# Row sums of a 64 MB tensor: which rows of DRAM the first and the last loads read

## The chip, the cores and the metric

The kernel runs on one core of a Trainium2 chip. The metric is the device time of one execution in microseconds (us), as the median of several runs; lower is better. "The profile" is a record of one execution by the hardware profiler. Engines are named as it names them: DVE is VectorE, ACT is ScalarE, POOL is GpSimd, SP is SyncE, which here only issues transfers (SPq is its queue, ACTq that of ScalarE).

## The reference

```
x: (32, 512, 1024) float32
return np.sum(x, axis=-1).astype(np.float32)      # (32, 512)
```

There are 32 x 512 = 16,384 rows of 1,024 numbers (4 KB each), and each is summed. 64 MB are read, 64 KB are written.

## The kernel before

The rows are spread over the 128 partitions of the on-chip memory, J = 128 rows to each. Two regions of DRAM are laid out differently. `x_a` is the first 2,048 rows: partition p has 16 neighbouring rows, so that partitions are 64 KB apart. `x_b` is the rest: partition p has LONG = 112 neighbouring rows, so that partitions are 448 KB apart. The outputs `out_a` and `out_b` follow the same split. `rows_from(j, n)` gives n rows of every partition from column j on: columns 0 to 111 are `x_b`, 112 to 127 are `x_a`. The tile `sums` (128 x 128) holds the sum of column j in its column j.

Loads come in this order, all of them issued by SP through `rows` (L191):

- first a short load of FIRST = 7 rows per partition, columns 96 to 102 of `x_b`. It is moved to the entry of the program by `issue_first_load_at_entry`.
- then seven loads of 16 rows, 8 MB each (`wholes`): the whole of `x_a`, then columns 0 to 95 of `x_b`. The buffer pool `in` has three buffers. The second load of all is held until ScalarE has done a first tiny activation (`ready`), the third until VectorE has summed the first seven rows (`first`).
- then the last nine rows, columns 103 to 111 of `x_b`: one load of 6 rows, one of 2, and the last row in two halves of 512 numbers (L236, L237).

VectorE sums the short load and the first six of the large ones with one `tensor_reduce` each (L152). The last large load and the nine last rows are summed row by row, by VectorE with an add of a row's two halves that accumulates (`halves`, L166) and by ScalarE with an accumulating copy (`act`, L179). The very last row is summed in two steps, as its halves arrive.

There are three stores (L202). Two are issued by ScalarE once VectorE is done with the load of two rows: `out_b` columns 0 to 95 (384 bytes per partition) and all of `out_a` (64 bytes per partition). The third is issued by SP at the very end: `out_b` columns 96 to 111 (64 bytes per partition, 448 bytes apart). `wait_for_the_store_at_the_clear` lets the closing round of the engines go ahead and has only GpSimd's clearing of the semaphores wait for this third store.

Of the kernel before, what the change touches and what calls it, by code (L numbers as in the profile page):

```python
# [100 lines left out]
@with_exitstack  # L101
def kernel(
    ctx: ExitStack,
    tc: tile.TileContext,
    x: bass.AP,
    out: bass.AP,
):
    nc = tc.nc
    nc.at_finalize(issue_first_load_at_entry)
    nc.at_finalize(order_waits)  # L110
    nc.at_finalize(wait_for_the_store_at_the_clear)
    fp32 = mybir.dt.float32
    P = 128
    batch, seq, dim = x.shape
    rows = batch * seq
    J = rows // P
    BIG = 16

    LONG = J - BIG
    rows_in = x.flatten_outer_dims()
    rows_out = out.rearrange("b s -> (b s)")
    x_a = rows_in[: P * BIG].rearrange("(p j) d -> p j d", p=P)
    x_b = rows_in[P * BIG :].rearrange("(p j) d -> p j d", p=P)
    out_a = rows_out[: P * BIG].rearrange("(p j) -> p j", p=P)
    out_b = rows_out[P * BIG :].rearrange("(p j) -> p j", p=P)


    def rows_from(j, n):
        return x_b[:, j : j + n, :] if j < LONG else x_a[:, j - LONG : j - LONG + n, :]

    last = LONG - BIG
    FIRST = 7
    pieces = (512, 512)
    LINE = 64

    with (
        tc.tile_pool(name="small", bufs=1) as smallpool,  # L140
        tc.tile_pool(name="in", bufs=3) as inpool,
        tc.tile_pool(name="unread", bufs=4, space=bass.MemoryType.PSUM) as upool,
        tc.tile_pool(name="stage", bufs=1) as stpool,
        tc.manual_schedule(),
    ):


        seed = smallpool.tile([P, LINE // 2], fp32)
        sums = stpool.tile([P, J], fp32)

        def vec(dst, src):
            return nc.vector.tensor_reduce(  # L152
                out=dst, in_=src, axis=mybir.AxisListType.X, op=mybir.AluOpType.add
            )

        def hold(inst, until, reason):
            tc.add_manual_dep(
                inst.ins,
                until.ins.name,
                mybir.DependencyInfo(mybir.DependencyClass.Sync, mybir.DependencyReason.DATA),  # L160
                reason=reason,
            )

        def halves(dst, src):
            n = src.shape[-1] // 2
            return nc.vector.tensor_tensor_reduce(  # L166
                out=src[:, :n],
                in0=src[:, :n],
                in1=src[:, n:],
                scale=1.0,  # L170
                scalar=0.0,
                op0=mybir.AluOpType.add,
                op1=mybir.AluOpType.add,
                accum_out=dst,
            )

        def act(dst, src, n):
            unread = upool.tile([P, dim], fp32)
            nc.scalar.activation(  # L179
                out=unread[:, :n],  # L180
                in_=src,
                func=mybir.ActivationFunctionType.Copy,
                accum_out=dst,
            )

        sums_of = []

        def rows(t, a, n, j, n_act, pairs=False):
            nv = n - n_act
            block = t[:, a * dim : (a + n) * dim].rearrange("p (n d) -> p n d", d=dim)  # L190
            load = nc.sync.dma_start(out=block, in_=rows_from(j, n))  # L191
            if pairs:
                for q in range(nv):
                    sums_of.append(halves(sums[:, j + q : j + q + 1], block[:, q, :]))
            else:
                sums_of.append(vec(sums[:, j : j + nv], block[:, :nv, :]))
            for q in range(nv, n):
                act(sums[:, j + q : j + q + 1], block[:, q, :], dim)
            return load

        def store(eng, dst, j0, j1):
            return eng.dma_start(out=dst, in_=sums[:, j0:j1])  # L202

        nc.vector.memset(seed[:, :1], 0.0)  # L204
        unread = upool.tile([P, dim], fp32)
        ready = nc.scalar.activation(  # L206
            out=unread[:, :1], in_=seed[:, :1], func=mybir.ActivationFunctionType.Copy
        )

        j = last  # L210
        t = inpool.tile([P, BIG * dim + LINE], fp32)
        rows(t, 0, FIRST, j, 0)
        first = sums_of[-1]
        wholes = [LONG, *range(0, last, BIG)]
        for k, at in enumerate(wholes):
            t = inpool.tile([P, BIG * dim + LINE], fp32)
            if k < len(wholes) - 1:
                load = rows(t, 0, BIG, at, 0)
            else:
                rows(t, 0, BIG, at, 7, pairs=True)  # L220
            if k == 0:
                hold(load, ready, "no second load while the first one's descriptors are made")
            if k == 1:
                hold(load, first, "no descriptors of later loads while the first ones start")

        t = inpool.tile([P, BIG * dim + LINE], fp32)
        rows(t, FIRST, 6, j + FIRST, 2, pairs=True)
        two = rows(t, FIRST + 6, 2, j + FIRST + 6, 1, pairs=True)
        a = BIG - 1

        j += a
        c, width = pieces
        whole = t[:, a * dim + c : BIG * dim + 2]
        nc.vector.memset(whole[:, width + 1 :], 0.0)  # L234
        part = t[:, a * dim : a * dim + c]
        nc.sync.dma_start(out=part, in_=rows_from(j, 1)[:, 0, :c])  # L236
        nc.sync.dma_start(out=whole[:, :width], in_=rows_from(j, 1)[:, 0, c:])  # L237
        late = "its packets come behind those of the loads"
        hold(store(nc.scalar, out_b[:, :last], 0, last), two, late)
        hold(store(nc.scalar, out_a, LONG, J), two, late)  # L240
        halves(whole[:, width : width + 1], part)
        halves(sums[:, j : j + 1], whole)
        store(nc.sync, out_b[:, last:], last, LONG)


# [28 lines left out]
```

## Time and profile before

| what | value |
|---|---|
| median of 3 runs | 161.25 us (161.15 to 161.28) |
| the profiled execution | 161.23 us |
| its span, first to last instruction | 159.4 us |
| DVE busy | 120.6 us, 76% of the span |
| ACT busy | 12.1 us, 8% |
| transfers | 2160 packets, 67.18 MB, mean 421 GB/s over the span |

The span is what the profile sees of the execution; the difference to the execution's own time, 1.8 us, lies outside it. Busy shares are over the whole span. A transfer is split over 16 DMA engines; a packet here is what one partition gets of one transfer. A line such as `t<-in_x_dram SPq DMA_DIRECT2D x1, 3584.0 KB, 10.8` is a transfer from DRAM into a tile, issued once by SP, with its size and the microseconds from its issue to its landing.

### The profile page before, as it was taken

The page shows a single profiled execution, that of the slowest core. Times are in us where ns is not written, and L with a number is a line of the kernel's source. Part 1 is how long each engine was busy: PE and PEld are TensorE (multiplying, and loading weights), DVE is VectorE, ACT ScalarE, POOL GpSimd, SP SyncE. Part 2 cuts the span into 40 slices and gives each one's busy share as a digit, 9 for nine tenths or more (in the row PEclk, how much of TensorE's full clock was granted, in tenths as well). Part 3 has the DMA queues.
Part 4 walks back from the last instruction along what each step waited for, and adds up shares of the span by engine and source line. Part 5 has one row for each costly group of instructions (what it writes and reads, how often), then busy time and mean ns, then how long its engine had stood idle before and what let it go on. Part 6 is the DMA issues. An engine that isn't in the chain of part 4 may idle for free.

```text
span 159.4 us, 135 instructions
## 1 busy us (share of the span) xinstructions
DVE 120.6 (76%) x41; ACT 12.1 (8%) x22; POOL 0.2 (0%) x4
## 2 busy tenths in 40 slices
DVE  0029600499985999779995899949999499994955
ACT  3000000000000000000000000000000000003993
POOL 0000000000000000000000000000000000000000
DMA  8999989699699699699699797996996996996983
GB/s 302 396 486 526 411 378 526 280 510 526 263 526 526 263 526 526 263 526 493 296 526 444 345 526 345 444 526 280 510 526 263 526 526 263 526 526 265 425 376 134
DMA packets 2160, 67.18 MB, mean 421 GB/s; under 512 B 624, under 2 KB 624, under 8 KB 880
## 3 DMA queue, kind: packets, MB, share of 16 engines
q1 hardware_dynamic: 1872, 67.12, 97.8%
q10 hardware_dynamic: 288, 0.06, 0.2%
HBM read 67.11 MB, written 0.07 MB: 421 GB/s over the span
## 4 chain that ended last, share of the span: by engine, by line
DMA 71%; DVE 27%; SPq 1%; issue 0%; DVEq 0%
DMA t<-in_x_dram 71%; DVE sums L152 26%; SPq L191 0%; SPq L236 0%; DVE t L166 0%; DVEq L269 0%
## 5 line engine op out<-in xcount | busy, mean ns | idle before, releaser
L152 DVE TENSOR_REDUCE sums<-t 128x16 f32<-128x16384 f32 (+1 forms) x7 | 110.9, 15848 | 32.3 <-DMA t<-in_x_dram 32.3
L179 ACT ACTIVATE unread<-t 128x1024 f32<-128x1024 f32 x10 | 10.1, 1010 | 144.2 <-DMA t<-in_x_dram 144.2
L166 DVE CUSTOM_DVE_ANT_0 t<-t 128x512 f32<-128x512 f32 (+2 forms) x16 | 9.6, 656 | 4.0 <-DMA t<-in_x_dram 4.0
L179 ACT ACTIVATION_READ_ACCUMULATOR unread<-t 128x1 f32 x10 | 1.9, 186 | 0.0
L206 ACT ACT_TABLE_LOAD x1 | 1.3, 1283 | 0.8 <-PEq L258 0.8
L166 DVE DVE_READ_ACCUMULATOR2_ANT sums<- 128x1 f32 x15 | 1.3, 84 | 0.0
L204 DVE MEMSET seed<- 128x1 f32 x1 | 0.1, 59 | 0.8 <-PEq L258 0.8
L206 ACT ACTIVATE unread<-seed 128x1 f32<-128x1 f32 x1 | 0.2, 174 | 0.0
L258 POOL MEMSET const-bfloat16-1.0<- 128x1 bf16 x1 | 0.1, 101 | 0.0
L258 POOL MEMSET const-uint8-127<- 128x1 uint8 x1 | 0.1, 101 | 0.0
L258 POOL MEMSET const-float32-0.0<- 128x1 f32 x1 | 0.1, 98 | 0.2 <-issue 0.2
L258 POOL MEMSET const-float32-1.0<- 128x1 f32 x1 | 0.1, 98 | 0.0
L166 DVE DVE_READ_ACCUMULATOR2_ANT t<- 128x1 f32 x1 | 0.1, 81 | 0.0
L234 DVE MEMSET t<- 128x1 f32 x1 | 0.1, 59 | 0.0
## 6 DMA issues: line engine op xcount, KB each, us to landing
t<-in_x_dram SPq DMA_DIRECT2D x1, 3584.0 KB, 10.8
t<-in_x_dram SPq DMA_DIRECT2D x1, 3072.0 KB, 28.7
t<-in_x_dram SPq DMA_DIRECT2D x1, 1024.0 KB, 30.8
t<-in_x_dram SPq DMA_DIRECT2D x2, 256.0 KB, 31.0
t<-in_x_dram SPq DMA_DIRECT2D x7, 40.7
out_dram<-sums ACTq DMA_DIRECT2D x1, 48.0 KB, 1.6
out_dram<-sums ACTq DMA_DIRECT2D x1, 8.0 KB, 1.7
out_dram<-sums SPq DMA_DIRECT2D x1, 8.0 KB, 1.4
```

What stands on the lines that cost most here:

```text
L152: return nc.vector.tensor_reduce(out=dst, in_=src, axis=mybir.AxisListType.X, op=mybir.AluOpType.add)
L166: return nc.vector.tensor_tensor_reduce(out=src[:, :n], in0=src[:, :n], in1=src[:, n:], scale=1.0, scalar=0.0, op0=mybir.AluOpType.add, op ...
L179: nc.scalar.activation(out=unread[:, :n], in_=src, func=mybir.ActivationFunctionType.Copy, accum_out=dst,)
L204: nc.vector.memset(seed[:, :1], 0.0)
L206: ready = nc.scalar.activation(out=unread[:, :1], in_=seed[:, :1], func=mybir.ActivationFunctionType.Copy)
L234: nc.vector.memset(whole[:, width + 1 :], 0.0)
L258: nc = _bacc.Bacc("TRN2", target_bir_lowering=False, num_devices=1)
```

## The change

The rows of a partition are cut into three regions of DRAM instead of two. The first seven columns are `x_f`, the first 896 rows of the tensor: partition p has 7 neighbouring rows, and partitions are 28 KB apart. The last nine columns are `x_l`, the last 1,152 rows: partition p has 9 neighbouring rows, and partitions are 36 KB apart. Between them lies `x_b`, as before with 112 rows a partition, 448 KB apart, and all seven large loads read it. The columns of `sums` are now in the order of the loads. The sizes and the order of the loads, the engines that sum the rows and the holds stay as they are.

There is again one store for each region: from ScalarE `out_b` (448 bytes per partition) and `out_f` (28 bytes per partition, end to end), and at the end from SP `out_l` (36 bytes per partition, end to end in one piece of 4,608 bytes).

```diff
-    LONG = J - BIG
+    FIRST, LATE = 7, 9
+    LONG = J - FIRST - LATE
     rows_in = x.flatten_outer_dims()
     rows_out = out.rearrange("b s -> (b s)")
-    x_a = rows_in[: P * BIG].rearrange("(p j) d -> p j d", p=P)
-    x_b = rows_in[P * BIG :].rearrange("(p j) d -> p j d", p=P)
-    out_a = rows_out[: P * BIG].rearrange("(p j) -> p j", p=P)
-    out_b = rows_out[P * BIG :].rearrange("(p j) -> p j", p=P)
-
+    x_f, x_b, x_l = (
+        rows_in[P * at : P * (at + n)].rearrange("(p j) d -> p j d", p=P)
+        for at, n in ((0, FIRST), (FIRST, LONG), (FIRST + LONG, LATE))
+    )
+    out_f, out_b, out_l = (
+        rows_out[P * at : P * (at + n)].rearrange("(p j) -> p j", p=P)
+        for at, n in ((0, FIRST), (FIRST, LONG), (FIRST + LONG, LATE))
+    )
+
+
+    late_at = FIRST + LONG
 
     def rows_from(j, n):
-        return x_b[:, j : j + n, :] if j < LONG else x_a[:, j - LONG : j - LONG + n, :]
-
-    last = LONG - BIG
-    FIRST = 7
+        if j < FIRST:
+            return x_f[:, j : j + n, :]
+        if j < late_at:
+            return x_b[:, j - FIRST : j - FIRST + n, :]
+        return x_l[:, j - late_at : j - late_at + n, :]
+
...
-        j = last
         t = inpool.tile([P, BIG * dim + LINE], fp32)
-        rows(t, 0, FIRST, j, 0)
+        rows(t, 0, FIRST, 0, 0)
         first = sums_of[-1]
-        wholes = [LONG, *range(0, last, BIG)]
+        wholes = range(FIRST, late_at, BIG)
...
-        rows(t, FIRST, 6, j + FIRST, 2, pairs=True)
-        two = rows(t, FIRST + 6, 2, j + FIRST + 6, 1, pairs=True)
+        a = BIG - LATE
+        rows(t, a, 6, late_at, 2, pairs=True)
+        two = rows(t, a + 6, 2, late_at + 6, 1, pairs=True)
         a = BIG - 1
 
-        j += a
+        j = J - 1
...
-        hold(store(nc.scalar, out_b[:, :last], 0, last), two, late)
-        hold(store(nc.scalar, out_a, LONG, J), two, late)
+        hold(store(nc.scalar, out_b, FIRST, late_at), two, late)
+        hold(store(nc.scalar, out_f, 0, FIRST), two, late)
         halves(whole[:, width : width + 1], part)
         halves(sums[:, j : j + 1], whole)
-        store(nc.sync, out_b[:, last:], last, LONG)
+        store(nc.sync, out_l, late_at, J)
```

## The prediction

> **What bounds the kernel now.** I read the page first, then a table of windows cut at the landings of the loads, then the transfers in a window at either end. Everything here is one profiled execution of 159.4 us span.
>
> The page, in parts 1, 3, 4 and 6 (engines: busy us, share, count; queues: packets, MB, share of 16 engines; the chain that ended last; transfers: size, us from issue to landing):
>
> ```profile
> DVE 120.6 (76%) x41; ACT 12.1 (8%) x22; POOL 0.2 (0%) x4
> ...
> q1 hardware_dynamic: 1872, 67.12, 97.8%
> ...
> DMA 71%; DVE 27%; SPq 1%; issue 0%; DVEq 0%
> ...
> t<-in_x_dram SPq DMA_DIRECT2D x1, 3584.0 KB, 10.8
> ...
> out_dram<-sums ACTq DMA_DIRECT2D x1, 48.0 KB, 1.6
> out_dram<-sums ACTq DMA_DIRECT2D x1, 8.0 KB, 1.7
> out_dram<-sums SPq DMA_DIRECT2D x1, 8.0 KB, 1.4
> ```
>
> The queue of the loads fills 97.8% of 16 DMA engines' span. VectorE's 27% of the chain is only the chain walking back through a buffer's release; the transfers run on under it, as the windows show (columns: window, length, busy DVE, ACT, POOL with counts, clock, DMA share, GB/s):
>
> ```profile
> 10.77:30.11 19.34, 7.62 (x1) 0.00 (x0) 0.00 (x0) 1.00 1.00 434
> 30.11:49.50 19.39, 17.22 (x1) 0.00 (x0) 0.00 (x0) 1.00 1.00 433
> 49.50:68.85 19.35, 17.22 (x1) 0.00 (x0) 0.00 (x0) 1.00 1.00 434
> 68.85:88.16 19.31, 17.22 (x1) 0.00 (x0) 0.00 (x0) 1.00 1.00 434
> ```
>
> Each window runs from one landing of a 16-row load to the next. The DMA share is 1.00 in all four and a reduction takes 17.22 us of 19.3: the DMA engines never pause, VectorE has about 2 us to spare per tile. So the time is (first packet) + (bytes at 434 GB/s) + (what the first and last packets lose) + (the work after the last landing). Only those ends can move the result, unless an address pattern changes the 434.
>
> The first end, the transfers from 0 to 3 us (40 slices of 0.075 us):
>
> ```profile
> DMA  0000000000000999900090000980000000809989
> ...
> DMA packets 30, 0.86 MB, mean 287 GB/s; under 512 B 0, under 2 KB 0, under 8 KB 0
> ```
>
> The first packet starts in slice 13, at 0.98 us. The first load's 3584 KB are 3.67 MB, which at 434 GB/s take 8.46 us. It lands at 10.77. After its last packet a transfer still takes 0.37 us to land (found below). So 10.77 - 0.98 - 8.46 - 0.37 = 0.96 us go missing when the stream starts. The trace's records of single packets say where: the first packet of each of the 16 engines takes 1.06 to 1.96 us, every later packet of the same 28,672 bytes 1.06 to 1.07. The engines that start early are the slow ones, and all 16 finish their first packet between 2.6 and 3.04 us.
>
> The other end, the last instructions in order of time (start, us):
>
> ```profile
> 157.25 0.43 DVE L166 CUSTOM_DVE_ANT_0 t<-t 128x257 f32<-128x257 f32 x1 [0.21 <-DMA t<-in_x_dram]
> 157.60 0.08 DVE L166 DVE_READ_ACCUMULATOR2_ANT sums<- 128x1 f32 x1
> 157.71 0.35 SPq L202 DMA_DIRECT2D out_dram<-sums  x1
> ```
>
> The last piece lands at 157.22, VectorE needs 0.45 us, the store is issued at 157.71. By the packet records its packets run from 158.55 to 158.76 and it lands at 159.13, 0.37 us after the last packet. Semaphore clearing ends the span at 159.44.
>
> **The change part by part.** Instruction for instruction nothing is added or removed: 12 loads of 128 descriptors with the same sizes in the same order (7, seven times 16, 6, 2 and two half rows), the same reductions, the same three stores on the same queues with the same holds. What moves is where in DRAM they read and write.
>
> *The seven 16-row loads.* Before, the first of them read `x_a`, where partitions are 64 KB apart; the other six read `x_b`, 448 KB apart. After, all seven are 448 KB apart. The table above has both: 19.34 us for the neighbouring region, 19.31 to 19.39 for the strided ones. Cost: 0.
>
> *The last nine rows.* Partitions go from 448 KB apart to 36 KB apart. Packet records: 24,576 bytes take 912 ns, 8,192 take 309, 2,048 take 84, with no spread at all within a load; these are the DMA engine's own times. The nearest rows again say that distance changes nothing in a running stream. Cost: 0.
>
> *The first seven rows.* Partitions go from 448 KB to 28 KB apart, in the one place where the stream is not yet steady. No row shows a cold start from neighbouring rows. From below: if the whole excess came from 16 engines asking for far-apart addresses at once, it goes: -0.96 us. From above: if neighbouring rows collide more than distant ones, I bound it by the excess once more, +0.96. The nearest rows are the 64 KB and 448 KB windows, which agree within 0.1 us, and they say 0; but they are warm. Also, the two engines that start last (at 1.90 and 1.97) have nearly undisturbed first packets, 1.14 and 1.06 us, and one of them is the last engine to finish the loads, at 156.88; the earliest finishes at 156.51. So healing the slow first packets of the early engines alone brings nothing; the late starts must move too. I take -0.1. Whatever is gained here arrives at the end one for one, since the engines run back to back.
>
> The Trainium skill, "DMA: Bandwidth & Descriptors", section "Latency and other measured facts", reports that rows a large power of two apart in HBM lower the rate: 207 GB/s per direction at 512 KiB against 214 with padding. 448 KB is no such power, and this trace shows 433 to 434 GB/s on either layout. If the page's 3% did apply to the first load, an estimate from it would be 0.03 x 8.46 = 0.25 us gained.
>
> *The stores on ScalarE's queue.* 384 bytes per partition become 448, and 64 become 28. Packet records: 22 ns for 384 bytes, 10.5 for 64, eight packets per engine, so well under 0.1 us either way. They are covered: SP looks at their semaphores from 158.11 on, and the round of all engines that follows is over at 158.80, while the clear waits until 159.13 for the last store. The second store lands at 158.07 and is looked at at 158.24, so its landing may slip by 0.17 + 0.33 = 0.5 us before it costs anything. Cost: 0; without the cover, its slip.
>
> *The last store.* This one has no cover: the clear waits for it. [...] The packets cannot cost more than now (84 ns per engine). [...] The second store has neighbouring 64-byte pieces and lands 0.37 us after its last packet, like the strided one, so neighbourhood alone is free. Upper bound: the 0.37 us doubled, +0.37. Lower bound: 9 columns instead of 16 save nothing that I can find beyond 0.05, half the packet time. I take +0.05.
>
> *Sum.* 159.44 - 0.1 + 0.05 = 159.4 us of span. The profiled execution took 161.23, 1.79 outside the span, and the median of the three runs is 161.25. 159.39 + 1.79 = 161.18, and with the 0.02 to the median 161.2. A measurement of this kernel can tell about 0.2%, 0.32 us, from no change, so this counts as no change.
>
> **The rivals.**
>
> *The start heals (faster).* The first packets slow each other because of their addresses. For it: the 16 first packets are slow together and recover together at 3.0 us, which looks like a shared resource rather than a fixed latency, since late starters take 1.06. Against it: two engines start 0.9 us late, and addresses in a steady stream make no difference. Half of the excess gives 161.25 - 0.48 = 160.75; all of it 160.3. The point from which it decides: all 16 engines must finish their first packet by about 2.7.
>
> [...] The Trainium skill, same page, section "Specifications", says that a transfer under 512 B is done by read-modify-write; all three stores are below that before and after, so by that rule alone nothing changes.
>
> *The start gets worse (slower).* 16 engines in one region of 3.5 MB collide where they were spread over 56 MB. Up to the excess again: half of it 161.7, all of it 162.2. Against it: `x_a`, 8 MB in one piece, runs at 434 GB/s.
>
> *The change does not do what it says.* Not plausible here: the diff changes plain address arithmetic, and the descriptors (128 pieces per transfer) have the same form as those of `x_a` and `out_a` now.
>
> **How the numbers follow.** No measurable change 0.42: the nearest rows all say zero. The healed start 0.33: it is the only large unexplained loss in the kernel, and the change touches it. The store's price over 0.32 us 0.15, the worse start 0.10, together 0.25. The likeliest case gives 161.2, with its own range of 160.95 to 161.55. The wide range takes in half of the healed start and more (160.5) and the doubled landing with some of a worse start (161.8); what lies beyond, a start healed by more than three quarters or worsened by more than half, is about 0.15 to 0.2.
>
> **What would show it.** The windows between landings of 16-row loads should stay at 19.3 us and 434 GB/s; if one moves, my claim on distance falls. The first load's landing, 10.77 now, is the test of the start: 10.7 as I have it, 10.3 or less for the faster rival, 11.2 or more for the worse start. [...] From the last load's landing to the store's issue 0.49 us should stay. If the span moves with all of these unchanged, the prediction was wrong in a way that I did not think of.

## The result and the profile after

The changed kernel takes 161.55 us (median of 20 runs, 161.32 to 161.76) against 161.19 us (20 runs, 161.10 to 161.42): a ratio of 1.002, 95% interval 1.0014 to 1.0026. It is slower by 0.36 us, small but clear of the noise. The forecast was no measurable change, at 161.2.

The profiled execution took 161.50 us with a span of 159.7. First the page's lines on transfers (size, us from issue to landing):

```profile
t<-in_x_dram SPq DMA_DIRECT2D x1, 3584.0 KB, 11.3
...
out_dram<-sums ACTq DMA_DIRECT2D x1, 56.0 KB, 1.6
out_dram<-sums ACTq DMA_DIRECT2D x1, 3.5 KB, 1.5
out_dram<-sums SPq DMA_DIRECT2D x1, 4.5 KB, 1.4
```

The first load lands at 11.3 instead of 10.8; the stores take what they took. The stream between the landings of large loads (window, length, busy engines, clock, DMA share, GB/s):

```profile
11.29:30.58 19.29, 7.62 (x1) 0.00 (x0) 0.00 (x0) 1.00 1.00 435
30.58:49.90 19.32, 17.22 (x1) 0.00 (x0) 0.00 (x0) 1.00 1.00 434
49.90:69.26 19.36, 17.22 (x1) 0.00 (x0) 0.00 (x0) 1.00 1.00 433
```

It is the same stream, between 0.07 us faster and 0.01 slower per load than the windows before, which took 19.31 to 19.39. The transfers of the first 3 us (40 slices of 0.075 us):

```profile
DMA  0000000000000999900000090000000000089899
...
DMA packets 27, 0.77 MB, mean 258 GB/s; under 512 B 0, under 2 KB 0, under 8 KB 0
```

27 packets have begun instead of 30. The trace's records of single packets show three engines that lag: their first packets take 2.30 to 2.42 us, where before the slowest took 1.96. All 16 engines were through their first packet at 3.04 before; now the last is at 3.54. And the end:

```profile
157.51 0.43 DVE L175 CUSTOM_DVE_ANT_0 t<-t 128x257 f32<-128x257 f32 x1 [0.19 <-DMA t<-in_x_dram]
157.87 0.08 DVE L175 DVE_READ_ACCUMULATOR2_ANT sums<- 128x1 f32 x1
157.98 0.35 SPq L211 DMA_DIRECT2D out_dram<-sums  x1
```

The first landing is 0.52 us late. The last piece is 0.27 us late (157.49 against 157.22), so about half of the delay is made up on the way. The trace also records when each of the 16 shares of a load lands. Three shares are late at the first load (11.07, 11.18 and 11.29 us, the thirteenth at 10.78; before, all four came within 0.02), and three are still late at the last piece (157.31, 157.41 and 157.49, the thirteenth at 157.16). From the last landing on, everything costs what it did (0.49 us to the store's issue, 1.42 to its landing, as before), and the span is 0.27 us longer.

### The profile page after: what moved, and what is told of

It reads as the page before. It is cut to its first block, busy times and chain, and to the rows that moved or that the text cites. A ratio compares the mean times of both kernels' runs of the same rounds, so it can differ in the third digit from the quotient of the medians.

```text
span 159.7 us, 135 instructions
## 1 busy us (share of the span) xinstructions
DVE 120.5 (75%) x41; ACT 12.1 (8%) x22; POOL 0.2 (0%) x4
## 4 chain that ended last, share of the span: by engine, by line
DMA 71%; DVE 27%; SPq 1%; issue 0%; DVEq 0%
DMA t<-in_x_dram 71%; DVE sums L161 26%; SPq L200 0%; SPq L245 0%; DVE t L175 0%; DVEq L278 0%
## 5 line engine op out<-in xcount | busy, mean ns | idle before, releaser
L188 ACT ACTIVATE unread<-t 128x1024 f32<-128x1024 f32 x10 | 10.1, 1011 | 144.5 <-DMA t<-in_x_dram 144.5
## 6 DMA issues: line engine op xcount, KB each, us to landing
t<-in_x_dram SPq DMA_DIRECT2D x1, 3584.0 KB, 11.3
```

The lines of the kernel that those rows point to most:

```text
L188: nc.scalar.activation(out=unread[:, :n], in_=src, func=mybir.ActivationFunctionType.Copy, accum_out=dst,)
```

## The experiments

**Which part costs.** The layout was made a list of regions in DRAM order, each with the columns it holds; loads, holds and the columns of the three stores stay as in the changed kernel.

```diff
-    x_f, x_b, x_l = (...)          # and out_f, out_b, out_l
+    for cols in REGIONS:
+        n = sum(hi - lo for lo, hi in cols)
+        src = rows_in[P * at : P * (at + n)].rearrange("(p j) d -> p j d", p=P)
+        dst = rows_out[P * at : P * (at + n)].rearrange("(p j) -> p j", p=P)
...
# changed kernel:     [[(0, 7)], [(7, 119)], [(119, 128)]]
# e1_first_only:      [[(0, 7)], [(7, 119), (119, 128)]]
# e2_last_only:       [[(0, 7), (7, 119)], [(119, 128)]]
# e3_one_region_16:   [[(0, 7), (119, 128)], [(7, 119)]]
# e4_first_elsewhere: [[(7, 119)], [(0, 7)], [(119, 128)]]
```

> Only the first seven columns are a region of neighbouring rows (28 KB apart); the other 121 columns are one region, 484 KB apart, the last nine included. Theory 'spacing' (the first load starts worse because its partitions lie close together): first load lands at about 11.3 us as in the changed kernel, time 161.5 us. Theory 'the end' (the nine neighbouring rows or the small stores cost it): first load still about 11.3 or not, but time 161.2 us.

Measured: 161.55 us (ratio to before 1.0020, interval 1.0011 to 1.0029), first load 11.19 in the profiled execution, as in all that follows. The changed kernel's whole loss is there with the first region alone.

> Only the last nine columns are a region of their own (36 KB apart, stored as 36 bytes end to end); the first seven are with the 112 others, 476 KB apart. Theory 'spacing': first load lands at about 10.8 us, time 161.2 us. Theory 'the end': time 161.5 us.

Measured: 161.31 us (1.0004, 0.9995 to 1.0013), first load 10.91. The last region and the 36-byte store cost nothing that this can tell: the interval ends at +0.21 us.

> The first seven and the last nine columns share the region of 16 columns, so that the first load's partitions are 64 KB apart (and the last ones' too); the seven large loads are all 448 KB apart. Theory 'spacing', if closeness as such is the cause: between the two kernels, first load at 10.9 to 11.2 us, time 161.3 to 161.5 us. Rival 'this distance alone' (28 KB is bad by its remainder, not by its size): first load at 10.8 us or less, time 161.2 us.

Measured: 161.33 us (1.0001, 0.9992 to 1.0010), first load 11.00. In between, so it decided little yet.

> As the changed kernel, but in DRAM the region of the first load stands behind that of the large loads (56 MB into the tensor) and not at its beginning. Theory 'spacing': no difference to the changed kernel, first load at 11.3 us, time 161.5 us. Rival 'place' (the beginning of the tensor is what is slow to start on): first load at 10.8 us, time 161.2 us.

Measured: 161.50 us (1.0016, 1.0007 to 1.0025), first load 11.06, 0.2 us short of what was expected. By the time, the loss goes with the layout, not with the place in the tensor.

**Is it the first transfer, or any start from rest?** The first load is made twice, with a standstill before the second one and before the two large loads behind it:

```diff
         rows(t, 0, FIRST, 0, 0)
         first = sums_of[-1]
+        t = inpool.tile([P, BIG * dim + LINE], fp32)
+        again = rows(t, 0, FIRST, 0, 0)
+        hold(again, first, "the stream stands still before the second start")
+        second = sums_of[-1]
...
-                hold(load, ready, ...)
+                hold(load, second, ...)
...
-                hold(load, first, ...)
+                hold(load, sums_of[-2], ...)
```

> The changed kernel, but the first load (28 KB apart) is made twice, the second time into another buffer once VectorE has summed the first, and the two large loads behind it are each held until the sum before them is done. So the DMA engines stand still and start again from rest three times: once more with 28 KB, twice with 448 KB. Its total time means nothing. Theory 'simultaneous start' (16 engines that begin together get in each other's way, the more the closer their addresses): the second load of seven rows has slow first packets like the first one, 1.6 to 2.4 us where 1.06 is undisturbed, and takes as long from issue to landing (11 us); the large loads lose less. Theory 'cold' (only the first transfer of the program is slow): the second one's packets take 1.06 us from the first on and it lands 10 us after its issue.

> The kernel before, with the same edit: starts from rest with 448 KB twice (seven rows), then with 64 KB and with 448 KB (16 rows). Total time means nothing. Theory 'simultaneous start': the second load of seven rows takes about as long from issue to landing as the first (10.8 us), and less than its counterpart that is 28 KB apart, by 0.3 to 0.5 us. Theory 'cold': both counterparts alike, about 10 us.

The chain of e5 (start us, us), then that of e6; the first two rows of each are the first load and its repetition:

```profile
0.00 11.04 DMA t<-in_x_dram
18.71 10.94 DMA t<-in_x_dram
```

```profile
0.00 10.76 DMA t<-in_x_dram
18.43 10.77 DMA t<-in_x_dram
```

Each start from rest pays again, and the near one pays more, by 0.17 us on the repetition; 0.3 to 0.5 was expected. "Cold" falls. By the packet records the 16-row loads started from rest have slow first packets too: up to 3.3 to 3.5 us where 2.42 is undisturbed, at 64 as at 448 KB.

**Which distances cost.** More layouts of the same kind, whole kernels:

```diff
# e7_pitch_128k:  [[(0, 23), (119, 128)], [(23, 119)]]
# e8_pitch_512k:  [[(0, 128)]]
# e11_pitch_92k:  [[(0, 23)], [(23, 119), (119, 128)]]
# e12_pitch_256k: [[(0, 55), (119, 128)], [(55, 119)]]
# e15_pitch_384k: [[(0, 87), (119, 128)], [(87, 119)]]
```

ScalarE's two stores are cut where the regions are cut.

> First load 128 KB apart (it shares a region of 32 columns with the first large load and the last nine columns), the other large loads 384 KB apart. If only closeness costs: like the kernel before, 161.2 us, first load at 10.8. If powers of two cost: above 64 KB's 161.33, 161.4 or more.

Measured: 161.24 us (1.0008, 0.9999 to 1.0017), first load 10.82: as the kernel before. The profiled execution was one of the longer ones, with 161.45 us, and its chain shows that not all of a loss lies in the start:

```profile
0.00 10.82 DMA t<-in_x_dram
...
126.12 31.32 DMA t<-in_x_dram
```

The last of these rows in the kernel before:

```profile
126.14 31.09 DMA t<-in_x_dram
```

The first landing is almost the same, but the last one comes 0.22 us later (157.44 against 157.22). By the packet records, packets of the six-row load near the end take up to 1.15 us here, where all took 0.91 before. They are not a matter of distance alone: e4 has some of up to 1.10 at 36 KB, the distance at which all of the changed kernel's take 0.91. What makes them slow is not shown.

> One region for all 128 columns, every load 512 KB apart, a power of two. If only closeness costs: 161.2 us, as far apart as it gets. If the rule of the Trainium skill, 'DMA: Bandwidth & Descriptors', section 'Latency and other measured facts', on row pitches of large powers of two holds here, the stream itself slows by some 3%: the windows between landings go from 19.3 to 19.9 us, and the time to 165 or 166.

Measured: 161.74 us (1.0032, 1.0020 to 1.0044), the worst plain layout. The loss is in the first load; the stream, at 512 KB throughout, does not slow. Chain and windows of e8:

```profile
0.00 11.40 DMA t<-in_x_dram
```

```profile
11.40:30.70 19.30, 7.62 (x1) 0.00 (x0) 0.00 (x0) 1.00 1.00 435
30.70:50.05 19.35, 17.22 (x1) 0.00 (x0) 0.00 (x0) 1.00 1.00 434
50.05:69.45 19.40, 17.22 (x1) 0.00 (x0) 0.00 (x0) 1.00 1.00 432
```

So closeness alone is wrong, and the 3% on the stream, worked out from the Trainium skill's rule in the expectation, do not show here.

> First load 92 KB apart (a region of 23 columns with the first large load), the rest 420 KB apart. If the cost falls with distance: between 64 KB's 161.33 and 128 KB's 161.24, so 161.3 us. If odd multiples of 4 KB cost whatever their size: 161.5 us.

Measured: 161.49 us (1.0016, 1.0008 to 1.0024), first load 11.59 in the profiled execution, which took 161.90. Closeness would have had 161.3. That execution is 0.41 us longer than this kernel's median, so single executions of one layout can differ by nearly as much as layouts do.

> First load 256 KB apart (64 columns), the other large loads 256 KB apart too. If the cost of 512 KB apart (161.74 us) comes from the power of two, half of it should show here: 161.4 to 161.5 us, first load at 11.0 or later. If it takes 512 KB or more: 161.2 us, or a little less than the kernel before if distances of a few hundred KB are the best there is.

Measured: 161.49 us (1.0017, 1.0008 to 1.0026), first load 11.01. In this kernel the stream loses a little as well: its 64 KB packets average 2.43 us in the last large load, 2.42 elsewhere (and up to 1.03 us instead of 0.91 in the six-row load behind it). Its last landing is 0.46 us later than the kernel before's, its first 0.24.

Then one execution with many starts. Ahead of the changed kernel's work, the same load of seven rows is made from rest again and again:

```diff
+        t = inpool.tile([P, BIG * dim + LINE], fp32)
+        met = smallpool.tile([P, 1], fp32)
+        for p, n in probes:       # partitions, rows from one partition to the next
+            src = rows_in[: p * n].rearrange("(p j) d -> p j d", p=p)[:, :FIRST, :]
+            block = t[:p, : FIRST * dim].rearrange("p (n d) -> p n d", d=dim)
+            nc.sync.dma_start(out=block, in_=src)
+            landed = vec(met[:p], t[:p, :2])
```

> Ahead of the changed kernel's work stand 39 loads of 7 rows per partition, each from rest (the next waits until VectorE has read from the one before): 13 distances from 28 to 512 KB, three times each, in shuffled order. Total time means nothing; what counts is each load's time from issue to landing. Theory 'closeness': 28, 32 and 36 KB take 11.2 to 11.4 us, and it falls to 10.8 by 128 KB, but for 512 KB. Theory 'remainders' (addresses that fall on the same part of the memory): no order by size, but the three repeats of a distance agree within 0.15 us. Theory 'chance': repeats of one distance differ as much as distances do, 0.5 us.

The chain of e13 shows each probe as a row (start us, us); these four are 512, 28, 128 and 448 KB:

```profile
44.98 11.29 DMA t<-in_x_dram
...
90.21 11.18 DMA t<-in_x_dram
...
112.70 10.74 DMA t<-in_x_dram
...
135.03 10.74 DMA t<-in_x_dram
```

All of them, as median of three (us from issue to landing), beside the whole kernels with that distance in the first load:

| distance, KB | probe | whole kernel, us |
|---|---|---|
| 28 | 11.18 | 161.55 (changed kernel, e1), 161.50 (e4) |
| 32 | 11.00 | |
| 36 | 10.97 | |
| 64 | 10.92 | 161.33 (e3) |
| 92 | 11.03 | 161.49 (e11) |
| 128 | 10.74 | 161.24 (e7) |
| 192 | 10.82 | |
| 256 | 10.97 | 161.49 (e12) |
| 384 | 10.72 | 161.35 (e15) |
| 448 | 10.74 | 161.18 to 161.25 (medians of before in the rounds with several runs) |
| 476 | 10.89 | 161.31 (e2) |
| 508 | 11.05 | |
| 512 | 11.29 | 161.74 (e8) |

Repeats of a distance lie within 0.27 us of each other, and mostly within 0.15, while distances differ by up to 0.57. So among the probes it is neither chance nor size: the neighbouring 28 KB and the remote 512 KB are the two worst, 508 is far and bad, 128 is near and good. That there is no order by size is what the theory of remainders had; its repeats within 0.15 us were missed at 36 and 192 KB, and that remainders are the reason is not shown. The medians of the whole kernels follow the probes: 161.22 plus (probe - 10.74) misses none of the measured ones by more than 0.16. A single execution can stray further, as e11's landing of 11.59 does from the probes' 10.92 to 11.08 at 92 KB. The probes ran on another chip than the whole kernels; the kernel before, executed once beside them, took 161.90 us, and why is not known.

The packet records of the same 39 probes say how a distance acts. A load lands 7.73 to 8.09 us (median 7.76) after its slowest engine has finished its first packet. At 64 KB alone all three lie above, at 7.86 to 7.97: there the first packets are done as early as at 448 KB (2.94 to 3.07 us), and the loss comes behind them. The mean time of the 16 first packets does not follow the distance: 1.54 to 1.60 us at 512 KB, 1.58 to 1.68 at 448. The last engine does: it is through at 3.54 us after issue at 512 KB, 3.36 to 3.46 at 28, 2.96 to 3.04 at 448.

**How much of it is any start's.**

> Ahead of the changed kernel's work stand 52 loads of 28 KB per partition from rest, on 1, 2, 4, 8 or 16 partitions, so that each of so many engines has one packet; with 16, at nine distances from 28 KB to 4 MB. Theory 'in each other's way': one engine's packet takes 1.06 us, 16 engines' take up to 2, the more the worse the distance. Theory 'latency of any start': 1.5 us or more even with one engine, and hardly longer with 16.

One engine alone needs 1.27 to 1.59 us for its first packet, in four probes at the same address, against 1.06 later. So 0.2 to 0.5 us is the price of beginning, with no other engine in the way. The rest of this probe went wrong as a design: packets take 1.55 to 1.67 us on average with two partitions, 2.6 to 2.8 with four and eight, and 2.9 to 3.3 with 16, at any distance. A slow receiving end would do this, but no run shows it by itself. The Trainium skill, "SBUF — State Buffer", section "Door 1: The DMA port swizzle", says that four neighbouring partitions share a port; that four packets of 28 KB take 3.3 us together, about 35 GB/s, hardly more than the 27 GB/s of one engine in the stream (28 KB in 1.06 us), goes with that. So these probes tell nothing of 16 engines that write to 128 partitions. Their landings do differ by distance, 5.6 to 5.7 us at 28 KB and 7.2 to 7.4 at 4 MB, but in an order unlike that of e13.

**Between the engines or inside one?** Two kernels lay the rows out in groups of four partitions, with one distance inside a group and another between groups:

```diff
+    def groups(v, lo, hi):                                  # e9_engines_apart
+        v = v.rearrange("(g r) d -> g r d", r=4 * N)[:, 4 * lo : 4 * hi]
+        return v.rearrange("g (i j) d -> g i j d", i=4)
...
+    def groups(v, lo, hi):                                  # e10_engines_close
+        v = v.rearrange("(i r) d -> i r d", i=4)[:, P // 4 * lo : P // 4 * hi]
+        return v.rearrange("i (g j) d -> g i j d", g=P // 4)
```

> First and last columns share a region of 16, laid out by groups of four partitions: inside a group the partitions of the first load are 28 KB apart as in the changed kernel, from group to group 256 KB as with 64 KB a partition. By the Trainium skill, 'DMA: Bandwidth & Descriptors', section 'The descriptor swizzle', a DMA engine takes four neighbouring partitions at a time, so a group is one engine's. Theory 'between engines' (what counts is how far apart the 16 engines begin): as 64 KB apart, first load at 11.0 us, time 161.3 us. Theory 'within an engine' (its own next packets too near): as the changed kernel, 11.2 to 11.3 and 161.5 us.

> The reverse: from group to group 28 KB, inside a group 2 MB from partition to partition. Theory 'between engines': the groups begin within 0.9 MB, closer than the 2.6 MB of the changed kernel: first load at 11.3 us or later, time 161.5 us or more. Theory 'within an engine': as the kernel before, 10.8 and 161.2 us.

Measured: 162.30 us (1.0064, 1.0052 to 1.0077) and 162.99 (1.0103, 1.0090 to 1.0116). Both inconclusive. The nested form starts its first packet at 1.44 and 1.42 us instead of 1.0, and the nested 36-byte store takes 1.8 and 2.4 us to land instead of 1.4; counted from the first packet, both first loads take 10.1 us. So the nested form was put into probes, read from the first packet on:

```diff
+            src = rows_in[: 32 * g].rearrange("(g r) d -> g r d", g=32)[:, : 4 * i]
+            src = src.rearrange("g (i j) d -> g i j d", i=4)[:, :, :FIRST, :]
```

> Probes as in e13, with nested layouts: groups of four partitions lie at one distance, the partitions of a group at another. To be read from each load's first packet to its landing, since the nested form starts later; plain 28, 448 and 512 KB are among them (10.23, 9.78 and 10.33 us by e13). Theory 'between engines': the distance from group to group decides; groups 1792 KB apart (as in plain 448 KB) take 9.8 us whatever lies inside, groups 2048 KB apart (as in plain 512 KB) 10.3, groups 128 KB apart (28 to 32 KB inside) 10.2. Theory 'within an engine': the distance inside decides, so that 28 KB inside takes 10.2 us at any distance of the groups.

| between groups, KB | inside: 28 KB | 64 KB | 256 KB | 448 KB | 508 KB | plain layout of that group distance |
|---|---|---|---|---|---|---|
| 2048 | 10.48 to 10.73 | 10.30 to 10.86 | 10.21 to 10.31 | 10.17 to 10.35 | 10.42 to 10.58 | 10.34 to 10.44 |
| 1792 | 9.89 to 9.94 | 9.80 to 10.02 | 9.85 to 10.09 | | | 9.81 to 9.87 |
| 512 | 9.88 to 10.25 | | | | | 9.74 to 9.83 |
| 256 | 9.94 to 10.06 | | | | | 9.95 to 9.97 |
| 128 | 10.02 to 10.07 | | | | | 10.02 to 10.08 |
| 112 | | | | | | 10.16 to 10.47 |

(us from the first packet to the landing, three probes each, four of plain 448 KB; the plain 128, 64 and 32 KB, for groups 512, 256 and 128 KB apart, are those of e13. With 444 KB inside and 1792 between groups the three probes took 9.78 to 9.83.) The rows of this table hold together and the columns do not: with 28 KB inside, a load is good when its groups are 1792 KB apart and bad when they are 2048 apart. Two of those probes in the chain, from issue, so with 1.3 us ahead of the first packet in both:

```profile
57.81 11.80 DMA t<-in_x_dram
...
151.44 11.23 DMA t<-in_x_dram
```

The first has 2048, the second 1792 KB between groups, both 28 KB inside. So the distance acts between groups, as the theory "between engines" had it; what lies inside adds 0 to 0.2 us at 28 KB by the middle one of three probes, and up to 0.5 in single probes. That a group is one engine's is what the Trainium skill states, "DMA: Bandwidth & Descriptors", section "The descriptor swizzle"; the trace has no column for it, so "between engines" rests on that page, "between groups of four partitions" on the runs.

**A better version?**

> First load 384 KB apart (a region of 96 columns with the first five large loads and the last nine columns), the last two large loads 128 KB apart. By the probes 384 KB lands at 10.72 us, 448 KB at 10.74: 161.2 us, no different from the kernel before. A rival that the large loads' distance matters too (as 256 KB seemed to in e12): 161.4 us or more, with the first load still at 10.7.

Measured: 161.35 us (1.0010, 1.0001 to 1.0019), single runs from 161.15 to 161.88, first load 10.85 in the profiled execution. No gain: none of the distances tried beats 448 KB, which the kernel before had.

## Why the prediction was wrong

*The stream.* Right for this change: the large loads at 448 KB run at 433 to 435 GB/s between their landings, and the last nine rows, 36 KB apart, land 10.97 us after the last large load, against 11.02 before. That the running stream never loses anything is too strong: the profiled executions of e4, e7 and e12 have slow packets near the end.

*The stores.* Right, with the terms near zero: the last store lands 1.42 us after its issue, as before, and its packets take 8 to 11 ns. No run shows the +0.05 taken for it: the two kernels do not differ here, and e2, which has the same last store, ends its interval at +0.21 us. A last store can land later, though, by more than the bound of +0.37. In e10, where neighbouring 36-byte pieces come from different groups, it lands 0.97 us after its last packet instead of 0.37, and in e13 the store with the changed kernel's own layout does so after 1.00, so that layout alone does not explain it. The cause was not taken apart.

*The first seven rows.* This is the step that failed. The prediction put -0.1 us, between bounds of -0.96 and +0.96, and gave as its reason that the nearest rows, steady loads at 64 and 448 KB, agree. It noted that those rows were warm and used them all the same. A steady stream says nothing of a start: e8 runs 512 KB at full rate in the stream and loses 0.55 us at the start, and a start at 64 KB, e3's distance, costs 0.18 us by the probes though the steady `x_a` ran at 434 GB/s. Measured, the term is +0.52 us at the first landing, +0.27 on the span, +0.36 on the medians. The prediction's own sign for the worse start, a first landing at 11.2 us or more, came up at 11.29.

*What carries a late start to the end.* The prediction had "one for one"; in the profiled pair about half of it came through. Other layouts keep more: against the kernel before, e8's first landing is 0.63 us late and its last 0.53, e11's 0.82 and 0.66, and the medians go with the probes nearly one for one. Why the profiled pair lost half is not shown. It was right that the latest engine decides: the probes give the landing as its first packet's end plus 7.76 us.

*The rivals.* "The start heals" named the right place and the wrong sign. "The start gets worse" was what happened, at 0.10, but its story, that neighbouring rows collide, is only the case at hand: 512 KB is as bad, 508 nearly so, and 128 KB is fine. The excess of 0.96 us that both were priced from was no measure of what a layout can do, since 0.2 to 0.5 us is paid even by one engine alone. (Half of it makes 160.77 for the healed start, not 160.75; nothing hangs on that.)

What stays open is the rule itself: why some distances make an engine late, and whether their remainders decide. The runs give the distances, not the cause.

## What to carry to other kernels

A steady transfer's price says nothing about its start: read the first packets of the first load by themselves, because a stream that never pauses passes much of its latest engine's delay on to the end (0.27 of 0.52 us here, 0.53 of 0.63 in e8). Where a load of this kind starts from rest, its layout in DRAM is worth 0.5 us, and neighbouring rows are not the safe choice; try a few distances, in one execution with repeated starts, and count each against the load's landing.

## What the runs showed of the hardware

- A load of 128 x 28 KB from rest takes 10.7 to 11.4 us to land in e13, by its distance, and repeats of a distance agree to 0.27 us. Single landings in other executions reach 11.59 (e11).
- A DMA engine that begins alone needs 1.27 to 1.59 us for 28 KB, and 1.06 once it runs.
- A nested address pattern of three terms starts its first packet 1.32 us after issue, a plain one 0.96 us.
- The stores of the two kernels, of 28, 36 and 64 bytes per partition, all land 0.37 to 0.38 us after their last packet. It isn't always so: e1's store of 448 bytes, 484 bytes apart, takes 0.88 where the changed kernel's, end to end, takes 0.40, and nothing waits for it there; the last stores of e10 and e13 take 0.97 and 1.00.
- Packets of the six-row load near the end of the stream (24 KB) all take 0.91 us in the kernels before and after, but up to 1.03 to 1.15 us in the profiled executions of e4, e7 and e12, with no one distance in common.
